# Softmax over 16,384 rows: the second load as one transfer of five rows instead of three transfers

## Chip, cores and metric

The kernel runs on one core of one Trainium2 chip. The metric is the device time of one execution in microseconds (us), the median of several runs. The time before the change is 160.05 us, the median of three runs (159.54 to 160.09).

## The reference

The input is 16 x 1024 x 512 float32 numbers, taken as 16,384 rows of 512. Each row is divided by 2 and turned into a softmax:

```python
x_scaled = x / 2.0
x_max = np.max(x_scaled, axis=-1, keepdims=True)
exp_x = np.exp(x_scaled - x_max)
return exp_x / np.sum(exp_x, axis=-1, keepdims=True)
```

So 33.55 MB are read from HBM and 33.55 MB are written.

## The kernel before

**Tiles.** The 16,384 rows are 128 rows for each of the 128 partitions of SBUF. They are cut into ten tiles of 3, 5, then eight times 15 rows per partition (`TILES`, L10). A row is 2,048 bytes, so a partition's part of tile 0 is 6,144 bytes, of tile 1 10,240 bytes, of a large tile 30,720 bytes, each contiguous in HBM and in SBUF. The arena in SBUF holds 98 rows per partition; tiles 8 and 9 lie where tiles 0 to 3 were, and are loaded when those have been stored (`LATE`, L18). Tiles 6 and 7, and 8 and 9, are stored by one transfer each (`BLOCKS`, L14), the others by one each, so there are eight stores; each tile has its own load.

**Compute.** ScalarE (ACT) takes the exponential of each row with its sum (L231 for tile 0, L301 in a loop for the rest). VectorE (DVE) takes the reciprocals of the sums (L191) and multiplies the rows by them in place (L194). The row's maximum is not subtracted; instead, at the end all sums are counted that lie between 1 and 1e30 (L205, L209, a matmul at L223, L213), and only if one does not would a second, slow pass run (L250 to L281). It does not run here.

**Queues and order.** Three engines issue transfers, each on a queue of its own; all run on the same 16 DMA engines.

- SyncE (SP) issues load 0 (L179), and all eight stores (L239 to L242). It waits for the multiplication of tile 2 (L238) before the first store, so that the stores begin when many loads have been queued.
- ACT issues load 1 (L180) and loads 2 to 7 (L182 to L184), all before its own computing.
- GpSimd (POOL) issues loads 8 and 9 (L202 to L204), when the stores that free their place have landed.

Loads 0 and 1 are placed by hand (L308 to L316) ahead of the drain with which each engine enters the start barrier; loads 2 to 7 come behind this barrier. TensorE (PE) waits for each load in turn (L218 to L221) and passes on to ACT how many chunks of rows may be taken (`s_go`, taken at L165).

**The second load.** `load` (L130) is one transfer for all tiles but tile 1 (`SPREAD`, L24). That tile is loaded by three transfers, which add 16 each to one semaphore: rows 0 to 3 of all 128 partitions, row 4 of partitions 0 to 125, and row 4 of partitions 126 and 127 (L135). PE waits until the semaphore shows 48 (L219).

Of the kernel before, what the change touches and what calls it, by code (L numbers as in the profile page):

```python
# [19 lines left out]

HEAD = [3]
E = 5

SPREAD = 1  # L24

FIRST = 2

# [7 lines left out]
def kernel(  # L35
# [5 lines left out]
    nc = tc.nc  # L41
# [6 lines left out]
    xf = x.flatten_outer_dims()  # L48
    of = out.flatten_outer_dims()
    N, D = xf.shape  # L50
    P = nc.NUM_PARTITIONS
# [20 lines left out]
    def span(ts):  # L72
        assert all(tiles[u][2] == tiles[t][2] + tiles[t][1] for t, u in zip(ts, ts[1:]))
        return tiles[ts[0]][0], sum(tiles[t][1] for t in ts), tiles[ts[0]][2]
# [3 lines left out]
    loaded = [span(ts) for ts in LOADS]  # L78

    def dram(ap, ts):  # L80
        b, r, _ = span(ts)
        first, rows, _ = next(span(us) for us in BLOCKS if ts[0] in us)
        assert first <= b and b + r <= first + rows
        block = ap[first * P : (first + rows) * P].rearrange("(p r) d -> p r d", r=rows)
        return block[:, b - first : b - first + r]

    def sb(ts):
        _, r, at = span(ts)
        return arena[:, at : at + r, :]
# [18 lines left out]
    ld = [nc.alloc_semaphore(f"ld{k}") for k in range(len(loaded))]  # L108
# [20 lines left out]

    def load(eng, k):  # L130
        ts = LOADS[k]
        r = loaded[k][1]
        parts = [(0, P, 0, r)]
        if k == SPREAD:
            parts = [(0, P, 0, r - 1), (0, 126, r - 1, r), (126, P, r - 1, r)]  # L135
        for p, q, lo, hi in parts:
            eng.dma_start(  # L137
                out=sb(ts)[p:q, lo:hi], in_=dram(xf, ts)[p:q, lo:hi]
            ).then_inc(ld[k], 16)

    stored_by = {j: s_home[k] for k, js in LATE.items() for j in js}
    for k, (_, r, at) in enumerate(loaded):
# [35 lines left out]
    def early():  # L178
        load(nc.sync, 0)  # L179
        load(nc.scalar, 1)  # L180

    def loads():  # L182
        for k in range(2, min(LATE)):
            load(nc.scalar, k)  # L184

    def program():

        for j, ks in enumerate(pairs):
# [3 lines left out]
                out=recip[:, b : b + c], in_=stats[:, b : b + c]  # L192
            )._wait_ge(s_exp, ks[-1] + 1).then_inc(s_rec, 1)
            nc.vector.tensor_mul(  # L194
                out=arena[:, a : a + c],
# [6 lines left out]
        for k, js in LATE.items():  # L202
# [3 lines left out]
            out=inside[:, :], in0=stats[:, :], scalar1=LO, scalar2=HI,  # L206
# [3 lines left out]
            out=inside[:, :], in0=inside[:, :], scalar=1.0, in1=stats[:, :],  # L210
# [3 lines left out]
            out=flag[:, :], in0=total[:, :], scalar1=float(N), scalar2=None, op0=Alu.is_ge,  # L214
# [1 line left out]


        for k, ts in enumerate(LOADS):  # L218
            nc.tensor.wait_ge(ld[k], 48 if k == SPREAD else 16).then_inc(  # L219
                s_go, sum(owner.count(t) for t in ts)  # L220
            )  # L221
        nc.tensor.wait_ge(s_ones, 1)
# [5 lines left out]
        for k, c in enumerate(HEAD):  # L228
            take(nc.scalar, s_go, 1)
            for b in range(starts[k], starts[k] + c):  # L230
                ins = nc.scalar.activation(  # L231
                    out=arena[:, b], in_=arena[:, b], func=Exp, scale=0.5,
# [86 lines left out]
    nc.switch_body(here, parent=None, valid_engines=[i.engine for i in jumps])  # L319
    loads()  # L320
    program()


# [28 lines left out]
```

## Time and profile before

| What | Value |
|---|---|
| median of three runs | 160.05 us (159.54 to 160.09) |
| the profiled execution's own time | 159.56 us |
| span of the profile, from the first instruction to the last event | 158.2 us |
| bytes moved, mean rate over the span | 67.11 MB, 424 GB/s |
| ACT busy | 80.4 us (51%) |
| DVE busy | 73.2 us (46%) |
| POOL, PE busy | 2.2 us, 0.2 us |
| packets on the DMA queues | 2,736 |

The span leaves out 1.36 us of the profiled execution's time. "Busy" is time in which an engine computes; issuing a transfer and waiting are not counted. A DMA packet is the contiguous piece of one partition; behind the pieces of a transfer, each DMA engine that took part writes a packet of 4 bytes, which reports to the semaphore. An ACT exponential of one row takes 0.61 us, a DVE multiplication of 15 rows 8.16 us.

### The profile page before, as it was taken

How to read it: one execution, taken by the hardware profiler on the slowest of the kernel's cores; microseconds unless marked ns; L12 is line 12 of the kernel's file. 1: busy time of each engine (PE TensorE's matmuls, PEld its weight loads, DVE VectorE, ACT ScalarE, POOL GpSimd, SP SyncE). 2: the span in 40 equal slices, each digit the busy share in tenths (PEclk: the TensorE clock that was granted, in tenths of full speed). 3: DMA queues.
4: the chain of work that ended last, by engine and by line, in shares of the span. 5: the costliest groups of instructions: out<-in, count | busy, mean ns of one | idle time of the engine just before them, and what ended most of it. 6: DMA issues, size and time to landing. Idle time of an engine off the chain costs nothing. (4 is left out here: it accounts for less than half of the span.)

```text
span 158.2 us, 657 instructions
## 1 busy us (share of the span) xinstructions
PE 0.2 (0%) x2; PEld 0.1 (0%) x2; DVE 73.2 (46%) x27; ACT 80.4 (51%) x257; POOL 2.2 (1%) x8
## 2 busy tenths in 40 slices
PE   0000000000000000000000000000000000000000
PEld 0000000000000000000000000000000000000000
DVE  0047003989989599199299000001991992000000
ACT  0590699999979849859700000597009930000000
POOL 0000000000000000000100100000000010000000
DMA  7998989899989989999999989998999996999695
GB/s 266 397 489 373 497 373 489 381 482 412 447 384 421 453 381 487 419 427 443 404 466 396 474 388 482 388 482 381 482 388 489 497 482 264 497 497 466 280 497 249
DMA packets 2736, 67.11 MB, mean 424 GB/s; under 512 B 304, under 2 KB 304, under 8 KB 688
## 3 DMA queue, kind: packets, MB, share of 16 engines
q1 hardware_dynamic: 1296, 34.34, 50.6%
q10 hardware_dynamic: 1152, 24.90, 37.0%
q0 software_dynamic: 288, 7.86, 11.5%
HBM read 33.55 MB, written 33.55 MB: 424 GB/s over the span
## 5 line engine op out<-in xcount | busy, mean ns | idle before, releaser
L301 ACT ACTIVATE arena<-arena x125 | 76.6, 614 | 41.9 <-ACTq L165 41.9
L194 DVE TENSOR_TENSOR arena<-arena,recip 128x7680 f32<-128x7680 f32 (+2 forms) x12 | 70.2, 5847 | 0.4
L191 DVE RECIPROCAL recip<-stats 128x15 f32<-128x15 f32 (+2 forms) x12 | 2.7, 224 | 57.9 <-ACT arena L301 48.8
L301 ACT ACTIVATION_READ_ACCUMULATOR arena<-arena x125 | 23.4, 187 | 0.0
L227 ACT ACT_TABLE_LOAD x1 | 1.3, 1283 | 5.8 <-issue 5.8
L137 POOL DMA_DIRECT2D arena<-in_x_dram x2 | 1.3, 630 | 85.8 <-DMA out_dram<-arena 85.8
L231 ACT ACTIVATE arena<-arena 128x512 f32<-128x512 f32 x3 | 1.9, 618 | 0.0
L205 POOL TENSOR_SCALAR inside<-stats 128x128 f32<-128x128 f32 x1 | 0.6, 629 | 38.4 <-ACT arena L301 38.4
L231 ACT ACTIVATION_READ_ACCUMULATOR arena<-arena 128x1 f32 x3 | 0.6, 187 | 0.0
L223 PE MATMUL total<-ones,count 128*1 128x1 f32 x2 | 0.2, 164 | 131.5 <-DVE inside L209 131.5
L209 DVE SCALAR_TENSOR_TENSOR inside<-inside,stats 128x128 f32<-128x128 f32 x1 | 0.3, 284 | 0.0
L213 DVE TENSOR_SCALAR flag<-total 1x1 int32<-1x1 f32 x1 | 0.1, 147 | 0.3 <-PE total L223 0.3
L223 PEld LDWEIGHTS total<-ones,count 128*1 128x1 f32 x2 | 0.1, 82 | 131.4 <-DVE inside L209 131.4
L200 POOL MEMSET ones<- 128x1 f32 x1 | 0.1, 98 | 2.2 <-POOLq L43 2.2
L336 POOL MEMSET const-float32-0.0<- 128x1 f32 x1 | 0.1, 104 | 0.2 <-issue 0.2
L336 POOL MEMSET const-bfloat16-1.0<- 128x1 bf16 x1 | 0.1, 107 | 0.0
L336 POOL MEMSET const-uint8-127<- 128x1 uint8 x1 | 0.1, 107 | 0.0
L336 POOL MEMSET const-float32-1.0<- 128x1 f32 x1 | 0.1, 104 | 0.0
L209 DVE DVE_READ_ACCUMULATOR inside<-inside,stats 128x1 f32 x1 | 0.1, 83 | 0.0
## 6 DMA issues: line engine op xcount, KB each, us to landing
arena<-in_x_dram ACTq DMA_DIRECT2D x6, 3840.0 KB, 36.3
out_dram<-arena SPq DMA_DIRECT2D x4, 3840.0 KB, 34.8
out_dram<-arena SPq DMA_DIRECT2D x2, 7680.0 KB, 40.2
arena<-in_x_dram POOLq DMA_DIRECT2D x2, 3840.0 KB, 26.2
out_dram<-arena SPq DMA_DIRECT2D x1, 1280.0 KB, 27.3
arena<-in_x_dram ACTq DMA_DIRECT2D x1, 1024.0 KB
arena<-in_x_dram SPq DMA_DIRECT2D x1, 768.0 KB, 5.6
out_dram<-arena SPq DMA_DIRECT2D x1, 768.0 KB, 15.2
```

The costliest lines, as they stand in the source:

```text
L137: eng.dma_start(out=sb(ts)[p:q, lo:hi], in_=dram(xf, ts)[p:q, lo:hi]).then_inc(ld[k], 16)
L191: nc.vector.reciprocal(out=recip[:, b : b + c], in_=stats[:, b : b + c])._wait_ge(s_exp, ks[-1] + 1).then_inc(s_rec, 1)
L194: nc.vector.tensor_mul(out=arena[:, a : a + c], in0=arena[:, a : a + c], in1=recip[:, b : b + c].unsqueeze(2).to_broadcast([P, c, D]),)._w ...
L200: nc.gpsimd.memset(ones[:, :], 1.0).then_inc(s_ones, 1)
L205: nc.gpsimd.tensor_scalar(out=inside[:, :], in0=stats[:, :], scalar1=LO, scalar2=HI, op0=Alu.max, op1=Alu.min,)._wait_ge(s_exp, len(sizes) ...
L209: nc.vector.scalar_tensor_tensor(out=inside[:, :], in0=inside[:, :], scalar=1.0, in1=stats[:, :], op0=Alu.mult, op1=Alu.is_equal, accum_ou ...
L213: nc.vector.tensor_scalar(out=flag[:, :], in0=total[:, :], scalar1=float(N), scalar2=None, op0=Alu.is_ge,)._wait_ge(s_tot, 1).then_inc(s_f ...
L223: nc.tensor.matmul(total[:, :], lhsT=count[:, :], rhs=ones[:, :], start=True, stop=True)._wait_ge(s_cnt, 2).then_inc(s_tot, 1)
L227: nc.scalar.preload_act_table(Exp)
L231: ins = nc.scalar.activation(out=arena[:, b], in_=arena[:, b], func=Exp, scale=0.5, accum_out=stats[:, b : b + 1],)
L301: ins = nc.scalar.activation(out=data, in_=data, func=Exp, scale=0.5, accum_out=stats[:, r : n_rows - E + 1 + r][:, bass.ds(now, 1)],)
L336: nc = _bacc.Bacc("TRN2", target_bir_lowering=False, num_devices=1)
```

## The change

All of load 1 becomes one transfer of five rows over 128 partitions, as the other loads are, and PE waits for 16 instead of 48. The lines of `load`:

```diff
-SPREAD = 1
...
     def load(eng, k):
         ts = LOADS[k]
-        r = loaded[k][1]
-        parts = [(0, P, 0, r)]
-        if k == SPREAD:
-            parts = [(0, P, 0, r - 1), (0, 126, r - 1, r), (126, P, r - 1, r)]
-        for p, q, lo, hi in parts:
-            eng.dma_start(
-                out=sb(ts)[p:q, lo:hi], in_=dram(xf, ts)[p:q, lo:hi]
-            ).then_inc(ld[k], 16)
+        eng.dma_start(out=sb(ts), in_=dram(xf, ts)).then_inc(ld[k], 16)
...
         for k, ts in enumerate(LOADS):
-            nc.tensor.wait_ge(ld[k], 48 if k == SPREAD else 16).then_inc(
+            nc.tensor.wait_ge(ld[k], 16).then_inc(
                 s_go, sum(owner.count(t) for t in ts)
             )
```

ACT issues two transfers fewer; every other instruction of every engine stays as it is and in its order, and the same bytes go to the same places.

## The prediction

> **What bounds the kernel.** First the page's row of DMA activity, its packets and its queues:
>
> ```profile
> DMA  7998989899989989999999989998999996999695
> DMA packets 2736, 67.11 MB, mean 424 GB/s; under 512 B 304, under 2 KB 304, under 8 KB 688
> q1 hardware_dynamic: 1296, 34.34, 50.6%
> q10 hardware_dynamic: 1152, 24.90, 37.0%
> q0 software_dynamic: 288, 7.86, 11.5%
> ```
>
> The three queues (SP, ACT, POOL) fill 50.6 + 37.0 + 11.5 = 99.1% of the 16 DMA engines' span. ACT and DVE are busy for about half of it. The chain of waits is no help: its last pieces end at 131.8 us, 26 us before the span does:
>
> ```profile
> 128.36 2.83 DVE arena L194
> 131.19 0.22 DVE inside L209 x2
> ...
> 131.68 0.15 DVE flag L213
> ```
>
> What follows is the last store. In SP's waits, the 26.6 us are the end of the kernel, the 90.7 us waits of the store queue for multiplications:
>
> ```profile
> SPq L162 <- DVE arena L194: 90.7, 4, 44.2
> SPq L162 <- DMA out_dram<-arena: 26.8, 1, 26.8
> SPq L287 <- DMA out_dram<-arena: 26.6, 1, 26.6
> ```
>
> None of these waits starves the DMA engines. The trace records each packet's start, duration, queue and size, though not its engine. On one engine a packet follows the one before at its duration less 3 ns, and each queue's sizes come in a fixed order; with these two rules I strung the 2,736 records into 16 rows, one per engine. Two engines whose times nearly coincide could be exchanged in this, so single rows are an inference; the groups below are not, since they differ in their sizes. The rows have no gap over 0.06 us, but for one of 0.25 us in one row. The last store was issued at 131.2 us, while the one ahead landed at 139.4 to 140.0: 8.2 us of cover.
>
> From start to start, packets take 81 ns (2,048 bytes), 306 (8,192), 382 (10,240), 1,135 (30,720), 2,264 (61,440); a report of 4 bytes takes 6. One engine's 67.11/16 = 4.194 MB at the last rate are 154.6 us of the 158.2. **So the end is that of the engine that finishes last**, and what counts is how load 1 divides its bytes and when each engine starts. By window, the packets that start at 1.0 to 1.3 us, 1.75 to 1.85, 157.1 to 157.55 and 157.55 to 157.8, in this order:
>
> ```profile
> DMA packets 14, 0.09 MB, mean 287 GB/s; under 512 B 0, under 2 KB 0, under 8 KB 14
> ```
> ```profile
> DMA packets 5, 0.03 MB, mean 307 GB/s; under 512 B 0, under 2 KB 0, under 8 KB 5
> ```
> ```profile
> DMA packets 14, 0.00 MB, mean 0 GB/s; under 512 B 14, under 2 KB 14, under 8 KB 14
> ```
> ```profile
> DMA packets 2, 0.00 MB, mean 0 GB/s; under 512 B 2, under 2 KB 2, under 8 KB 2
> ```
>
> Fourteen engines start at 1.01 to 1.26 us; the last two only at 1.783 and 1.804 (among the five packets of the second window). At the end, fourteen write their last report up to 157.52, two more at 157.70 and 157.77. Strung together:
>
> ```
>                       first packet  2 KB packets  first 30 KB packet  it is longer by  end
> two late engines      1.78, 1.80    none          6.38, 6.46          0.60, 0.51       157.30, 157.52
> twelve                1.01 to 1.26  9 each        6.46 to 7.02        0.19 to 0.30     157.16 to 157.77
> two                   1.01, 1.10    10 each       6.63, 6.64          0.28, 0.29       157.43, 157.44
> ```
>
> "It is longer by" compares with 1,138 ns, the usual duration. The two engines that start late are those without a packet of row 4: 126 rows over fourteen engines are nine each, and the two rows left go to two of these. The late engines lose 0.5 to 0.8 us at the start and are spared 9 x 81 + 6 = 735 ns, so they end among the rest.
>
> [...]
>
> **The change, step by step.** One engine's time for load 1:
>
> - before, late engines: 8 x 306 + 6 = 2,454 ns;
> - before, twelve: 2,454 + 9 x 81 + 6 = 3,189; the other two: + 81 + 6 = 3,276;
> - after, all: 8 x 382 + 6 = 3,062 (382 from the store of tile 1, the only transfer with 10,240-byte packets).
>
> So the late two get +608 ns, twelve -127, two -214. With all else kept, the late two end at 157.30 + 0.61 = 157.91 and 157.52 + 0.61 = 158.13, and the last of the others at 157.77 - 0.13 = 157.64. The end moves from 157.77 to 158.13: **+0.36 us**.
>
> Two terms are not shown by before. First, the stall on the first 30 KB packet. For 10,240 followed by 30,720 the nearest row is the late engines' own 8,192 followed by 30,720: 0.51 and 0.60 us; the others, after 2,048-byte packets, show 0.19 to 0.30. Both late rows come to the same moment (6.38 + 0.60 and 6.46 + 0.51 are 6.97), which may be a time before which that packet can't flow; arriving 0.61 later, they would then lose only what the others lose. Bounds: no stall on them, -0.60 of the +0.61; all of it kept, +0.36 at the end. If the others took on the late rows' stall they would end at 157.64 + 0.28 = 157.92, still ahead of 158.13. I keep the stall. Second, the late start itself, bounded from vanishing (the last of the others then ends the kernel, -0.13) to a second delay of the same size (a rival below).
>
> ACT's two dropped issues took 0.664 and 0.244 us, the second ending at 1.495. The first issue ended at 0.517, so ACT enters the start barrier 0.98 us earlier; SP drains by 0.557 and holds nothing back. Everything behind the barrier comes up to 0.98 us earlier:
>
> ```profile
> 0.00 0.38 SPq L137 DMA_DIRECT2D arena<-in_x_dram  x1
> 0.13 5.62 ACTq L137 DMA_DIRECT2D arena<-in_x_dram  x9
> 5.78 1.28 ACT L227 ACT_TABLE_LOAD   x1 [5.78 <-issue]
> 7.08 0.63 ACT L231 ACTIVATE arena<-arena 128x512 f32<-128x512 f32 x1
> ```
>
> Seven issues stay of ACT's nine; loads 2 to 7, the table load and the first exponential (to 6.1) move up; load 0 has landed by 5.6. That is worth nothing: ACT would only wait longer for load 2, which landed at 16.8 us (it idled 5.05 us before it), and load 2 comes when the DMA engines have moved what is ahead of it. It is hidden by load 1's bytes, which keep the engines at work until 6.4 or later; without this cover it would be worth up to 0.98. No wait is added; PE's 16 for 48 waits for the same bytes, and behind it PE only waits for later loads. Stores begin when tile 2 is multiplied (34.9 us), with load 2's landing up to 0.4 later; queued loads cover that to 68.5, and the last store has its 8.2.
>
> Sum: +0.36 us. Against the profiled execution, 159.56 + 0.36 = 159.92; this execution is 0.49 under the median, so the same step from the median gives 160.05 + 0.36 = **160.4**.
>
> **Rivals.** Half a per cent (0.80 us) is about what a measurement of this kernel can tell from no change.
>
> 1. *The stall is absorbed* down to what the others lose (0.28 instead of 0.51 to 0.60): the late two end at 157.60 and 157.90, +0.13, 160.2. For it speaks the common moment 6.97; against it that no such transition is in the trace.
> 2. *The late start goes with the extra transfers.* The late first packets come 0.29 us behind the end of ACT's third issue (1.495); if that issuing held them back, all engines start alike and all save 0.13: 159.9. Against it: the 126-row transfer does not use these engines at all.
> 3. *Slower: the late two fall back a second time.* ACT's six large issues now begin at 1.68 instead of 2.66, so before the late first packets at 1.78. If issuing elsewhere is what delays them, they can lose 0.52 again (1.783 against 1.260): 0.36 + 0.52 = +0.88, 160.9. It decides over half a per cent once they lose over 0.44 more. Against it: nothing shows a delay repeated.
> 4. *Faster: the cost per transfer is on the path.* If what follows the barrier sets the end, 0.98 goes: 159.1. Against it: small packets follow each other without gaps, at 81 ns. [...]
>
> **How the numbers follow.** The forecast 0.47, rival 1 0.20, rival 2 0.15, rival 3 0.13, rival 4 0.05. Within half a per cent are the forecast and rivals 1 and 2: 0.82; slower 0.13; faster 0.05. The range goes from rival 2 (159.9) less half the spread of the runs (0.55/2) to rival 3: 159.65 to 160.95; it leaves rival 4 out, and part of rival 3.
>
> **What would show it.** Right: 14 packets of 6,144 bytes at 1.0 to 1.3 us and two more engines near 1.8; no 2,048-byte packets, 144 records fewer (2,592); the last two reports 0.3 us or more behind the rest. If all sixteen end within 0.5 us, rival 1 or 2 holds, told apart by the first packets. A gap in the rows between loads 1 and 2, or late engines beyond 2.2 us at the start, would make the prediction wrong.

## The result, and the profile after

The changed kernel takes 160.72 us (median of seven runs, 160.28 to 161.41), the kernel before 159.54 us (seven runs, 159.47 to 160.09). The ratio is 1.0061, with a 95% interval of 1.0044 to 1.0079: 0.97 us slower (0.70 to 1.26); the bare medians differ by 1.18. The forecast was +0.36 us; the time lies in the range of 159.65 to 160.95, and the loss is just over the half per cent that the text took as the bound.

The page of the changed kernel, its row of DMA activity, packets and queues:

```profile
DMA  7999999999999899989899999999999999899992
DMA packets 2593, 67.11 MB, mean 421 GB/s; under 512 B 289, under 2 KB 289, under 8 KB 545
q1 hardware_dynamic: 1296, 34.34, 50.2%
q10 hardware_dynamic: 1008, 24.90, 36.7%
q0 software_dynamic: 288, 7.86, 11.7%
```

ACT's queue (q10) has 144 packets fewer for the same bytes, as forecast; one of the 2,593 is an instruction fetch. The DMA engines are as full as before until the last slice, which is at 2 tenths where it was at 5: fewer engines are at work there. The packets that start at 1.0 to 1.3, 1.7 to 1.76, 157.3 to 158.2 and 158.5 to 159.1 us, in this order:

```profile
DMA packets 14, 0.09 MB, mean 287 GB/s; under 512 B 0, under 2 KB 0, under 8 KB 14
```
```profile
DMA packets 5, 0.03 MB, mean 512 GB/s; under 512 B 0, under 2 KB 0, under 8 KB 5
```
```profile
DMA packets 14, 0.00 MB, mean 0 GB/s; under 512 B 14, under 2 KB 14, under 8 KB 14
```
```profile
DMA packets 2, 0.00 MB, mean 0 GB/s; under 512 B 2, under 2 KB 2, under 8 KB 2
```

Again fourteen engines start by 1.24 us, and two at 1.72 and 1.75 (among the five). At the end fourteen write their last report by 158.15 us, and two only at 158.64 and 158.99. By the rows strung together, these two are the late starters, and no exchange of rows that coincide makes them others. In before no engine stands apart at the end, and there it can't be told which ends are the late starters': rows that coincide can be exchanged so that the late two end anywhere from 157.16 to 157.70.

The issues and ACT's start (start, duration):

```profile
0.12 4.46 ACTq L130 DMA_DIRECT2D arena<-in_x_dram  x7
...
4.61 1.28 ACT L218 ACT_TABLE_LOAD   x1 [4.61 <-issue]
...
16.96 0.63 ACT L292 ACTIVATE arena<-arena  x1 [5.40 <-ACTq L156]
```

The table load comes 1.17 us sooner, and tile 2, the first large one, begins at 16.96 instead of 17.13: ACT waits 5.40 us for its load instead of 5.05. The line of before:

```profile
17.13 0.63 ACT L301 ACTIVATE arena<-arena  x1 [5.05 <-ACTq L165]
```

The end of the chain of waits, and SP's waits:

```profile
129.36 2.83 DVE arena L185
132.19 0.22 DVE inside L200 x2
...
132.68 0.15 DVE flag L204
```
```profile
SPq L153 <- DVE arena L185: 89.1, 4, 44.7
SPq L153 <- DMA out_dram<-arena: 27.3, 1, 27.3
SPq L278 <- DMA out_dram<-arena: 26.8, 1, 26.8
```

Compute ends 1.0 us later than before and the wait for the last store is as long as it was (26.8 against 26.6): compute follows the transfers.

**Where the time came from.** The rows of the engine that ends last, in us (for before, one of the rows that fit its records equally well):

```
                                    before (a twelve)   after (a late one)   difference
first packet                              1.26                1.72             +0.46
bytes of load 1                           3.19                3.06             -0.13
packets longer than usual, to 9 us        0.97                0.45             -0.53
the same, 9 to 45 us                      0.10                0.49             +0.39
the same, 45 to 60 us                     0.16                0.20             +0.03
the same, from 60 us on                   0.15                1.14             +1.00
last report ends                        157.77              158.99             +1.22
```

The first three rows make -0.20. The loss is in packets that take longer on the late engine, most of all one of 30 KB of POOL's queue, at 89.1 us, with 1,889 ns instead of 1,138, and one of ACT's queue at 66.0 us with 361 ns more. The median engine changes from 157.75 to 157.96 (by the landing of the last store). The last landing moves from 158.17 to 159.33, and 0.95 of these 1.16 us is the distance of the last engine from the median.

### The profile page after: what moved, and what is told of

Same layout as the page of the kernel before. It is cut to its first block, busy times and chain, and to the rows that moved or that the text cites. A ratio compares the mean times of both kernels' runs of the same rounds, so it can differ in the third digit from the quotient of the medians.

```text
span 159.4 us, 655 instructions
## 1 busy us (share of the span) xinstructions
PE 0.2 (0%) x2; PEld 0.1 (0%) x2; DVE 73.2 (46%) x27; ACT 80.4 (50%) x257; POOL 2.2 (1%) x8
## 2 busy tenths in 40 slices
DMA packets 2593, 67.11 MB, mean 421 GB/s; under 512 B 289, under 2 KB 289, under 8 KB 545
```

## The experiments

The main theory, **balance**: two engines start half a microsecond late, and the last engine sets the end; before spared the two 18 KB each. Rivals: the *times* of the issues and of the start barrier; the number of small transfers; something about all engines alike. Each experiment was timed in five rounds beside before on the same chip, and the ratios are to before.

| Kernel | ratio, interval | median at load 2 | last two at 35 us | last two at 76 us | median at the end | last two at the end |
|---|---|---|---|---|---|---|
| before | 1 | 16.52 | 0.25, 0.28 | 0.12, 0.35 | 157.75 | 0.34, 0.42 |
| the change | 1.0061 (1.0044-1.0079) | 16.01 | 0.49, 0.61 | 0.97, 1.00 | 157.96 | 1.02, 1.37 |
| e0, the change again | 1.0054 (1.0037-1.0071) | 15.95 | 0.46, 0.50 | 0.67, 1.15 | 157.98 | 1.17, 1.18 |
| e1, row 4 in two halves | 1.0045 (1.0029-1.0062) | 16.68 | 0.35, 0.69 | 0.45, 0.57 | 157.73 | 1.41, 1.51 |
| e2, cut on load 2 | 0.9998 (0.9978-1.0017) | 16.48 | 0.20, 0.26 | 0.18, 0.30 | 157.74 | 0.28, 0.51 |
| e3, cut on load 7 | 1.0027 (1.0009-1.0046) | 16.03 | 0.45, 0.55 | 0.09, 0.22 | 157.83 | 0.33, 1.05 |
| e4, one engine spared | 1.0048 (1.0026-1.0069) | 17.41 | 0.40, 0.56 | 0.41, 0.57 | 158.38 | 0.58, 0.60 |
| e5, two rows on load 1 | 1.0043 (1.0030-1.0056) | 17.42 | 0.24, 0.38 | 0.23, 0.34 | 158.44 | 0.34, 0.43 |
| e6, before, late loads on ACT | 1.0018 (1.0008-1.0029) | 16.55 | 0.31, 0.46 | 0.19, 0.30 | 158.37 | 0.48, 0.64 |
| e7, change, late loads on ACT | 1.0036 (1.0023-1.0049) | 16.02 | 0.45, 0.54 | 0.82, 0.96 | 157.79 | 0.93, 0.97 |
| e8, two others overloaded | 1.0101 (1.0085-1.0116) | 16.85 | 1.31, 1.34 | 1.31, 1.32 | 158.76 | 1.96, 2.02 |
| e9, repaired in the last store | 1.0037 (1.0023-1.0051) | 16.04 | 0.40, 0.44 | 0.57, 0.62 | see text | see text |
| e10, two rows on load 2 | 1.0036 (1.0023-1.0050) | 17.11 | 0.21, 0.21 | 0.20, 0.26 | 158.29 | 0.18, 0.53 |
| e11, three spared on load 2 | 1.0020 (1.0010-1.0029) | 16.87 | 0.12, 0.13 | 0.13, 0.21 | 157.98 | 0.29, 0.84 |

Columns after the ratio are from one profile each, in us: each transfer of all 128 partitions reports sixteen landings, one per engine (288 packets of 4 bytes for the eighteen transfers of the change); "median" is the middle of the sixteen, "last two" how far the two latest are behind it, for load 4 (35 us), the third store (76 us) and the last store (the end). Four of the profiled executions are not near the median of their kernel: e4's is 0.40 us under it, e9's 0.32 under, e6's 0.39 over, and e8's 1.00 over (162.34, the slowest of its five).

### Bytes or times: e0 to e3

e0 is the change unaltered. e1 to e3 are before with other cuts:

```diff
e1 -            parts = [(0, P, 0, r - 1), (0, 126, r - 1, r), (126, P, r - 1, r)]
e1 +            parts = [(0, P, 0, r - 1), (0, 64, r - 1, r), (64, P, r - 1, r)]
e2 -SPREAD = 1
e2 +SPREAD = 2
e3 -SPREAD = 1
e3 +SPREAD = 7
```

> The changed kernel again, as the reference for the runs beside it. If its loss is a property of the kernel and not of the chip it ran on, it stands 0.4 to 0.8% over before (ratio 1.0061 with 1.0044 to 1.0079 the first time), and in its packets two engines again start at about 1.7 us and end last, 0.5 us or more behind the median of the sixteen.

Measured 1.0054: the loss is the kernel's. But it is three engines that end together, 1.13, 1.17 and 1.18 us behind the median: the late two and, with them, a third; at 35 us the third-latest landing was 0.32 behind. In the change the third-latest was 0.49 behind at 35 us and 0.52 at the end, so a lag does not always grow.

> Load 1 stays three transfers, issued at the places of before, but row 4 is cut at 64 and 64 partitions instead of 126 and 2, so that all sixteen engines should carry the same bytes. Balance theory (the two late-starting engines decide the end, and before was faster because they were spared 18 KB): as slow as the change, 160.3 to 160.9 where before is 159.5 to 160.0, with the two late engines last. Rival, the issuing theory (the third transfer and the later start barrier of before are what helped, by their times and not by the bytes): as fast as before, within 0.2%.

Measured 1.0045: as slow as the change, with before's three transfers at before's places, and a start barrier still later than before's (POOL's memset behind it starts at 3.47 us, in before at 2.65, in the change at 1.57). The packets that start at 157.1 to 157.8 and at 158.7 to 159.0 us in e1:

```profile
DMA packets 14, 0.00 MB, mean 0 GB/s; under 512 B 14, under 2 KB 14, under 8 KB 14
```
```profile
DMA packets 2, 0.00 MB, mean 0 GB/s; under 512 B 2, under 2 KB 2, under 8 KB 2
```

Fourteen engines end by 157.73, as in before, and two over a microsecond later. This is the loss by itself. The issuing theory falls: what had changed are 16 KB more on the late two, and one or two small pieces fewer on each of the others. Both halves of row 4 run on all sixteen engines (e1's page has 320 packets of 4 bytes, the change's transfers 288). Neither the two halves nor the one transfer is faster (1.0045 and 1.0054), and both lose against the unequal cut.

> Load 1 is one transfer as in the change; the last row of load 2 is cut at 126 and 2 partitions instead, behind the start barrier. Balance theory: the two late engines are spared the same 18 KB, 9 us later, and the time is that of before within 0.2%. Issuing theory: the start barrier and the first loads are those of the change, so the time is that of the change, 0.4% or more over before.

Measured 0.9998: all of the loss is gone, with load 1 and the start barrier of the change: load 1 lands 7.2 us after its issue (7.4 in the change), and POOL's memset behind the barrier starts at 1.58 us (1.57). All sixteen last reports of e2 start within 157.1 to 157.85 us:

```profile
DMA packets 16, 0.00 MB, mean 0 GB/s; under 512 B 16, under 2 KB 16, under 8 KB 16
```

> The cut of 126 and 2 is on the last row of load 7, whose packets come at 58 to 68 us. Balance theory in its plain form (a constant lag is carried to the end, and it does not matter where it is taken off): as before within 0.2%. Balance with growth (the lag of the two engines grows where load and store queues alternate, 1.4 us at the end of the change's profile from 0.5 at 34 us): part of it stays, 0.2 to 0.4% over before. Issuing theory: as the change, 0.4% or more over before.

Measured 1.0027, half of the loss, between the two forms of the theory as the form with growth has it. But the engine that ends last here, 1.05 us behind, is by its row not a late starter. No engine was over 0.22 behind at 76 us, and by the rows that fit best the late two end at 0.13 and 0.31. So a lag taken off late is taken off, but another engine lost time on the way.

### Which engine, how much, whose queue: e4 to e7

```diff
e4 +            parts = [(0, P, 0, r - 1), (0, 120, r - 1, r), (120, P, r - 1, r)]
e5 +            parts = [(0, P, 0, r - 2), (0, 126, r - 2, r), (126, P, r - 2, r)]
e6, e7, without POOL's loads at L201 to L204
-        exponentials(straight, n_rows)
+        at = [straight, 93, 98, n_rows]
+        for (k, js), a, b in zip(LATE.items(), at, at[1:]):
+            exponentials(a, b)
+            nc.scalar.wait_ge(s_home[k], landings(js))
+            load(nc.scalar, k)
+        exponentials(at[-2], n_rows)
```

On how many engines a transfer runs shows in its packets of 4 bytes, one from each engine. The change has 288 for eighteen transfers of 128 partitions, sixteen each; before has sixteen more for its 126 and 2 partitions, by the rows fourteen and two; e1 has 32 more for its 64 and 64. In these cases the count is the largest divisor of the partitions up to 16. For the 120 and 8 partitions of e4, and the 104 and 24 of e11, the expectations estimate from it; their counts are not shown here.

> Row 4 of load 1 is cut at 120 and 8 partitions. If a transfer runs on the largest number of engines up to 16 that divides its partitions, fifteen engines take 8 packets each and eight of them one more, and only the last engine is spared; the other late one carries its full share. Balance theory, the end is that of the slowest single engine: nearly as slow as the change, 0.3 to 0.6% over before, with one engine alone at the end instead of two. If instead the mean load or the number of small packets counts, half or more of the loss goes: 0.0 to 0.25%.

Measured 1.0048, as the theory has it, but its runs go from 159.76 to 161.14, and its profile shows another cause beside it: the median engine reaches the end of load 2 at 17.41 instead of 16.52 us, and the last two are only 0.58 and 0.60 behind at the end. Inconclusive.

> The cut of 126 and 2 is made on the last two rows of load 1, so the two late engines are spared 37 KB, twice as much as in before, and come about 0.8 us ahead; the other fourteen carry some 0.13 us more than in before. Balance theory: an engine that is early costs nothing, so 0.0 to 0.2% over before. Rival, any departure of single engines from the rest (early as well as late) grows and costs: 0.3% or more over before.

Measured 1.0043: the expectation missed, and the profile shows that it was not by a lag. The sixteen are close together at the end (last two 0.34, 0.43), but their median is 0.69 later. It was lost in load 1: while the two spared engines had gone on to load 2, the 4 KB pieces of the others took 212 ns in the mean and up to 392, where the quickest took 158, and their first 30 KB packets 0.25 to 0.78 us more than usual.

> Before, with loads 8 and 9 issued by ACT between its exponentials instead of by POOL. It is the partner of the next run. The loads come at about the same times (77 and 89 us), so before's time within 0.3%.

> The change, with loads 8 and 9 issued by ACT in the same way. If the late engines' lag grows from 0.5 to over 1 us because of packets of POOL's queue (in the profiles, single 30 KB packets of that queue were 0.3 to 0.8 us longer on the late engines at 88 to 94 us), this run stands only 0.1 to 0.3% over its partner. If the growth comes with any load that alternates with stores, it stands 0.4 to 0.7% over, as the change does over before.

Measured 1.0018 and 1.0036: 0.0018 apart, as expected if POOL's packets make the growth. The pair is not clean, however: e6 lost time in another place (its median engine ends 0.62 us later than in before, by late loads that took longer). In e7 itself the lag grew to 0.96 by 76 us, before any late load, and then no more. So POOL's queue is not all of the growth; part comes where ACT's loads alternate with the first stores. The two shares were not separated.

### Other engines, other repairs: e8 to e11

```diff
e8, on load 2
+            parts = [
+                (0, P, 0, r - 2), (0, 126, r - 2, r - 1), (126, P, r - 2, r - 1),
+                (0, 80, r - 1, r), (80, 94, r - 1, r), (94, P, r - 1, r),
+            ]
e9, the change, in store(), for the last store alone
+            parts = [(0, P, 0, r - 2), (0, 126, r - 2, r), (126, P, r - 2, r)]
e10, on load 2
+            parts = [(0, P, 0, r - 2), (0, 126, r - 2, r), (126, P, r - 2, r)]
e11, on load 2
+            parts = [(0, P, 0, r - 1), (0, 104, r - 1, r), (104, P, r - 1, r)]
```

Not shown: `SPREAD` is 2 in e8, e10 and e11; PE waits until the semaphore of the cut load shows 96 in e8, and the end of e9 waits for the 32 more that its two added transfers add.

> All bytes are the same, but two other engines are given too many. On load 2, row 13 is cut at 126 and 2 partitions (which spares the late two, as in the run with the cut on load 2, equal to before), and row 14 at 80, 14 and 34: by the rule of the largest divisor the 34 partitions fall to two engines, 17 packets of 2 KB each. These two get 33 small packets, twelve get 15, the late two 5. Balance theory: the overloaded two end 18 x 81 ns = 1.46 us behind the twelve, less 0.1 for their early start, so 0.6 to 1.1% over before, with two engines alone at the end. Rival (something about the two late-starting engines themselves, or about many small transfers, makes the loss): within 0.3% of before.

Measured 1.0101, the largest loss, with the bytes of before. The page's rows of DMA activity and of POOL's queue in e8, and the packets that start at 160.2 to 160.5 us:

```profile
DMA  7999799999999899999999999999989699969990
...
q0 software_dynamic: 288, 7.86, 11.7%
```
```profile
DMA packets 2, 0.00 MB, mean 0 GB/s; under 512 B 2, under 2 KB 2, under 8 KB 2
```

The last slice is at 0: hardly an engine is at work in it. Two engines alone end 1.96 and 2.02 us behind the median; at 35 us it was 1.31 and 1.34, of the 1.36 worked out from small packets. The 80, 14 and 34 partitions have 32 packets of 4 bytes together, as sixteen, fourteen and two engines would give: e8 has 336, 48 over the change, and sixteen of these are those of the 126 and 2. The late starters are not special: two others that get more bytes end last. That their lag grew from 1.3 to 2.0 is shown for this one execution, the slowest of five; and 1.01 us of its later end is that of the median, which the theory does not give.

> The change, but the last store is cut: 28 of its 30 rows for all partitions, the last two rows for 126 and for 2. The late engines are spared 37 KB (1.4 us) in the very last transfer, nothing before. Balance theory: what counts is only the sum at the end, and the grown lag of 1.0 to 1.5 us is taken off there; the fourteen get 0.15 us more, so 0.0 to 0.3% over before and 0.3 to 0.5% under the change. If the change loses by anything else than the late engines' sum (earlier start barrier, first packets, waits of stores for late loads), it stays 0.4 to 0.7% over.

Measured 1.0037, just between the two expectations. No engine stands apart at the end: the last sixteen landings follow each other from 157.8 to 158.58 us, against 159.33 for the last in the change. What stays is the fourteen engines' larger share (0.15 us by the expectation) and more: by the rows, the median engine ends 0.30 later than in before. Some of the loss came back, but the intervals of e9 and of the change overlap, so how much isn't settled.

> The cut of 126 and 2 on the last two rows of load 2. It settles the run with two rows on load 1, whose 0.43% came with some 0.9 us lost by all engines within the first 9 us and with no engine far behind the rest. Balance theory: early engines cost nothing, the fourteen carry 0.13 us more than before, 0.0 to 0.2% over before. If departures to either side cost, 0.3% or more.

> The last row of load 2 cut at 104 and 24 partitions, which by the rule of the largest divisor spares the last three engines, the two late ones and the next (0.3 us behind the median, and among the last in the profiles of before and of the cut on load 2). Balance theory: the last engine comes 0.1 to 0.3 us sooner, the others carry up to 0.2 us more, so -0.1 to 0.1% against before: the best of these versions if any, and not to be told from before.

Measured 1.0036 and 1.0020: both above what was expected. In both the early engines made no lag at 35 and 76 us, but the median was 0.59 and 0.35 us late at the end of load 2, with small pieces that took longer again (4 KB: 208 ns in the mean against 159; 2 KB: 96 against 84; in e2 it was 85.5). So in these three kernels sparing an engine more than it is late did cost. The early engines made no lag; the time went with small pieces that took longer. That the engines which were ahead made them so is argued, not shown: in e1, which spares no engine, the 2 KB pieces took 104 ns in the mean. No version was faster than before.

## Why the prediction was right, and where its sum was not

- **What bounds the kernel: right.** The end is that of the engine that finishes last. e1 (fourteen engines as in before, two late, 1.0045), e2 (0.9998) and e8 (two other engines, 1.0101) show it.
- **The bytes of load 1: right.** No 2 KB packets, 2,592 of the queues; e8's lag at 35 us is what small packets of 81 ns give. That all sixteen engines share the new transfer, eight packets of 10,240 bytes each, was the sum's estimate, and no run had shown it; the change shows it, with sixteen reports of load 1 and eight such packets in each of the sixteen rows (403 ns in the mean, 385 in the store of tile 1).
- **The late start stays: right.** 1.72 and 1.75 us. So rival 2 falls, and rival 3 too, as it is not later than in before (1.78 and 1.80), though load 2 was issued 1.08 us sooner, and loads 3 to 7 at least that. The last two reports came 0.49 and 0.84 us behind the rest, as the prediction had asked.
- **The cost of transfers is hidden: right**, rival 4 falls: ACT's first compute came sooner (6.55 us, 7.08 in before) and waited longer for load 2 (5.40 us, 5.05), and the median engine ended later, not sooner (157.96, 157.75). One detail was off without harm: load 0 had not landed by 5.6 but by 6.35 us, so the first exponential began at 6.55 and not at 6.1.
- **The stall on the first 30 KB packet: wrong.** It was kept at 0.51 and 0.60 us on the late engines; in the change it is 0 on fifteen engines and 0.05 on one, though these packets started from 6.33 us on, so there is no moment before 6.97 at which that packet can't flow. In the prediction's own sum the late two would then have ended at 157.31 and 157.62 and the others by 157.36: about -0.15 us instead of +0.36. Over the fourteen profiles the stall goes with the small pieces: in the five kernels that cut load 1 (before, e1, e4, e5, e6) the packets of load 2 lost 0.31 to 0.68 us per engine before 9 us, in the nine others at most 0.01.
- **The slack of 0.25 us: not shown.** The sum took 157.30 and 157.52 as the ends of the late two in before. Its groups differ in their packets of load 1 alone, so behind load 1 their rows are an inference too: others fit as well, with ends from 157.16 to 157.70, and give +0.14 to +0.54 in place of +0.36.
- **"With all else kept": wrong, and this is the term that was mis-sized.** An offset at load 1 isn't carried unchanged over 150 us. First, the stall was put off and not saved. The mean time by which one engine's 30 KB load packets exceeded 1,138 ns:

```
                 to 9 us   9 to 60 us   from 60 us, POOL's queue
before             0.31       0.30           0.01
the change         0.00       0.55           0.39
e0                 0.01       0.69           0.45
e1                 0.33       0.16           0.14
e2                 0.00       0.61           0.01
e8                 0.00       0.95           0.54
```

  In before, e1 and e2 the first two columns add to 0.5 to 0.6, whichever comes first; the change, without a stall at load 2, got one at 38 to 55 us. Second, the last engine's lag grew, from 0.50 to 0.69 at 35 us to 1.18 to 1.51 at the end (the change, e0, e1), in e8 from 1.3 to 2.0. The forecast of +0.36 was 0.61 us of bytes less 0.25 of slack; in the first three the lag added 0.7 to 0.8 to itself on the way. In the profiles with two engines over 0.4 us behind the median at 76 us and the late loads on POOL's queue (the change, e0, e1, e8, e9, e4) the last column is 0.14 to 0.54 in five and 0.00 in e4; in before and e2 it is 0.01, and in e5 and e10 0.00 and 0.07, but in e3 and e11, without such a lag, 0.17. So it goes with the lag, though not strictly.

So the direction and the mechanism were right. The size was not: the two wrong terms had opposite signs, and the range held the time by luck, since its upper end came from rival 3, which did not happen. The chances gave 0.82 to within half a per cent; 0.61% falls to the 0.13 for slower, though the interval reaches to 0.44%.

**What stays open:** why load packets take longer on an engine that is behind. It goes mostly, not always, with a lag and comes where loads alternate with stores, and e7 shows that part of it isn't POOL's queue. Why the first large packets stall behind small pieces, and why two engines start late, wasn't tried.

## What to carry to other kernels

When the queues keep all sixteen DMA engines full (99.1% of the span in before), string the packets by engine and look at who ends last: here bytes moved off that engine counted (e2, 0.9998), fewer transfers and earlier issues did not (e0, 1.0054). Spare a late engine by about as much as it is late, and do it early: here one row in fourteen shares of nine on load 1 or load 2 was worth 0.5 to 0.6%, on load 7 half of it, and two rows lost most of it again. An offset of single engines should not be carried through a sum as a constant; in the change, e0 and e1 that of the last engine about doubled, from 0.50 to 0.69 us at 35 us to 1.18 to 1.51 at the end.

## What the runs showed of the hardware

- In all fourteen profiles the landings of the first load have two engines 0.42 to 0.68 us behind the median, and by the packets of before and the change it is their first packet that comes late (1.72 to 1.80 us, against 1.01 to 1.26).
- Small pieces at the end of load 1 or 2 took longer than elsewhere: those of 4 KB 212 and 208 ns in the mean (e5, e10; up to 392), against 159 in the last store (e9); those of 2 KB 85 to 109 in the mean, against 84 on load 7 (e3).
- Where load 1 ended in small pieces, the first 30 KB packets of load 2 took up to 1,921 ns (e5) instead of the usual 1,138.
- A 30 KB load packet took up to 2,340 ns (e0, POOL's queue, 87.3 us) where loads alternated with stores; stores' packets hardly changed (0.01 to 0.05 us per engine in total).
